# Hybrid decoder block on one core: the first two modulation vectors by quarters instead of halves

## The chip, the cores and the metric

The kernel runs on one core of a Trainium2 chip. The metric is the time of one execution in device microseconds (us). One matmul engine (TensorE, PE in the profile, its weight loads apart as PEld), VectorE (DVE), ScalarE (ACT) and GpSimd (POOL) work side by side; SyncE (SP) issues nearly all transfers.

## The reference

One block of a decoder in float32: 512 tokens of width 1024. What concerns this case is its head:

```python
mod = jax.nn.silu(c) @ w_ada[l] + b_ada[l]
shift1, scale1, gate1, shift2, scale2, gate2 = jnp.split(mod[:, None, :], 6, axis=-1)
h = rms_norm(x, norm1_w[l]) * (1.0 + scale1) + shift1
proj = h @ w_in[l]
aq, ak, av, gq, gk, gv, gg, glr = jnp.split(proj, split_points, axis=-1)
...
mixed = jnp.concatenate([att, go], axis=-1) @ w_out[l]
x = x + gate1 * mixed
```

`c` is one vector of 1024, `w_ada` is 1024 x 6144. `proj` feeds sliding-window attention (8 heads, window 128) and a gated linear attention (GLA, 4 heads, chunks of 64, decays from `glr` by a rank-16 gate). Behind them stand a product-key expert layer with 16384 experts, which takes most of the kernel's time, and a last norm.

## The kernel before

x stays in row blocks of 128 tokens (`gv` and the first half of `Eg`, `xn`); the projections need h transposed, [1024 rows of features, 512 tokens], in 8 blocks `k` of 128 features. Every float32 operand of a projection is split into a high and a low part (`hTh`, `hTl`; `wi_0h`, `wi_0l` for weight blocks 0 to 3, `wi_1h`, `wi_1l` for 4 to 7; `hilo`, L55: ScalarE copies the high part, VectorE subtracts) and each product is three matmuls (`mm3`, L63, lines 64 to 66).

The start-up does this. SP loads x in 8 pieces, then the matrices. ScalarE squares and sums x (L233), `rstd_of` (L71) takes the root on ScalarE and VectorE, ScalarE scales x (L237), and PE transposes it into banks `xt` (L246). `mod_half(v, half)` (L255) makes half of modulation vector 1 (scale) or 0 (shift): it loads 512 output columns of all 8 k blocks (1 MB twice; for v=1 into the ring `raw` of three buffers of 1 MB, for v=0 into `qT` and four `mixA`, which are free then), VectorE multiplies block k by silu(c)'s column k and adds (L267 for the first, L269 for the next 7, into `macc`), four matmuls with a column of ones sum over partitions (L273, into `mt`), and VectorE adds the bias (L275, `modT`) and, for v=1, forms (1+scale) times the norm's weight (L278, `aT`). With both vectors of a half there, four blocks of h follow: ScalarE applies scale and shift (L298; block 7 on VectorE, L300) and copies the high part (L301), VectorE takes the low part (L302). The order is (1,0), (0,0), four h, (1,1), (0,1), four h.

Behind it come the projections, in this order of the program: `decays` (L351: pglr, 16 wide, then `pz` by `gup`, then `la`), projection 3 (gq), projection 4 (gk), projection 0 (queries); one projection has two banks `pj` of 24 matmuls, and pglr has one. Then GLA's preparation (`gla_prep`, L427: 14 products on `Eg`, L451 and L452, then `kl`, L456), attention, projections 5 to 8 (`proj_N`, banks `pn`) between them, and the vectors 2 to 4 (`mod_part`, L202, also through the ring `raw`).

The order of each engine's instructions is not the program's: the tile framework schedules them with a simulated timeline (L38) that has its own durations, so an edit here can turn rows round further on. PSUM tiles come from tags: `m` and the pair `sc2` (`bank2`, L120, one buffer of two banks), `pt`, `po`, and `ph` (`pbank`, L123). A weight load of a projection is issued when its place in the ring of three is free, and SP's queue is taken in order.

Of the kernel before, what the change touches and what calls it, by code (L numbers as in the profile page):

```python
# [41 lines left out]
def peer_block_kernel(ctx: ExitStack, tc: tile.TileContext, a: dict, out: bass.AP):  # L42
# [186 lines left out]
    for n in range(NT):  # L229
        sq = frA.tile([P, D], F32, tag="m4", bufs=2, name=f"sqa{n}")  # L230
        ss = frA.tile([P, 2], F32, tag="ss", bufs=2, name=f"ssa{n}")
        for q in range(2):
            nc.scalar.activation(sq[:, q * 512:(q + 1) * 512], xn[n][q], AF.Square, accum_out=ss[:, q:q + 1])  # L233
        nc.vector.tensor_tensor(ss[:, 0:1], ss[:, 0:1], ss[:, 1:2], OP.add)
        r = rstd_of(frA, ss[:, 0:1], float(D), 1, f"ra{n}")
        for q in range(2):
            nc.scalar.activation(xn[n][q], xn[n][q], AF.Copy, scale=r)  # L237
    xts = []

    def x_transposes(ks):  # L240
# [67 lines left out]
    nc.vector.tensor_tensor(wgl, wg, wgh, OP.subtract)  # L308
    bcast_load(sink, a["sinks"], 8)
# [257 lines left out]
    proj_T(4, [[t[:, :, j, :] for t in gk] for j in range(2)], bank)  # L567
# [523 lines left out]
def layouts(inp):  # L1091
# [6 lines left out]
    o["w_ada"] = c(g["w_ada"][0])  # L1098
# [49 lines left out]
```

## Time and profile before

| | before |
|---|---|
| median of 3 runs (lowest to highest) | 1559.18 us (1557.12 to 1560.58) |
| the profiled execution | 1555.13 us |
| its span in the profile, mean granted clock | 1553.4 us, 0.99 |
| busy: PE, DVE, ACT, POOL | 1493.2, 1251.8, 688.8, 412.9 us |
| the first weight of a modulation vector summed | 13.80 us |
| first matmul of a projection (pglr) | 33.79 us |
| first matmul of projection 0 | 68.22 us |

All times below are from the start of the span. In a row of the timeline the first number is the start of a piece of work, the second what it lasted, in brackets how long the engine was idle before and what ended that. Two or more like instructions in a row share one line with their count; a float32 matmul of one column appears as two records (four matmuls are x8).

### The profile page before, as it was taken

What the parts mean: (1) busy time and instruction counts of PE and PEld (TensorE: products, weight loads), DVE (VectorE), ACT (ScalarE), POOL (GpSimd) and SP (SyncE); (2) the same over time, 40 slices, a digit from 0 to 9 for tenths busy, and PEclk for the clock granted to TensorE, in tenths of its full rate; (3) what the DMA queues carried; (4) which work ended last, traced back from release to release, by engine and by line L of the source; (5) the groups of instructions that cost most, each with busy time, mean ns of one, the idle gap of its engine ahead of it and who ended that gap; (6) DMA issues with size and microseconds to landing.
All of it is one profiled execution on the core that took longest, in us unless ns stands there. A gap on an engine that the chain in (4) does not pass through costs nothing.

```text
span 1553.4 us, 24408 instructions
## 1 busy us (share of the span) xinstructions
PE 1493.2 (96%) x9379; PEld 1328.2 (86%) x9379; DVE 1251.8 (81%) x2476; ACT 688.8 (44%) x1078; POOL 412.9 (27%) x327
## 2 busy tenths in 40 slices
PE   4999989899999999999999999999999999999996
PEld 3787878888998999999888888888888888888885
DVE  7578668589989898995678778878888878887997
ACT  5545576433445666564333333333333333333343
POOL 1000000144500000003243334433434434434550
PEclk9999999999999999999999999999999999999998
DMA  9253444262346677679998999888998989898893
GB/s 349 89 204 131 171 142 173 108 239 92 127 155 188 198 239 235 201 239 388 380 348 317 339 348 346 322 340 333 364 330 329 338 340 354 326 340 334 292 331 129
DMA packets 154932, 409.67 MB, mean 264 GB/s; under 512 B 10288, under 2 KB 77120, under 8 KB 142400
## 3 DMA queue, kind: packets, MB, share of 16 engines
q1 hardware_dynamic: 108736, 261.30, 47.2%
q0 software_dynamic: 36864, 134.23, 23.0%
q10 hardware_dynamic: 9216, 12.59, 2.2%
q8 instruction: 73, 1.20, 0.3%
q14 instruction: 43, 0.35, 0.1%
HBM read 366.14 MB, written 41.94 MB: 263 GB/s over the span
## 4 chain that ended last, share of the span: by engine, by line
PE 63%; DVE 3%; DMA 2%; ACT 1%; issue 1%; DVEq 0%; ACTq 0%; SPq 0%
PE acc L65 11%; PE acc L64 11%; PE acc L66 11%; PE ph L66 8%; PE ph L64 8%; PE ph L65 8%; PE pg L874 4%; DMA Gd<-gs 1%; DMA gr<-Gd 1%; DVE o L867 1%; ACT gs L876 0%; DVE o L862 0%; DVE oh L819 0%; DVE oh L822 0%; DVE oh L817 0%
## 5 line engine op out<-in xcount | busy, mean ns | idle before, releaser
L887 POOL DMA_INDIRECT gu<-in_u_dram,ix_u x128 | 170.2, 1329 | 531.5 <-PE pg L874 273.5
L897 POOL DMA_INDIRECT gv<-in_vP_dram,ix_v x128 | 171.0, 1336 | 214.9 <-DVE gu L889 183.1
L902 DVE SCALAR_TENSOR_TENSOR gacc<-gv,hg,gacc 128x1024 f32<-128x1024 f32 x127 | 162.7, 1281 | 3.3 <-DMA gv<-in_vP_dram,ix_v 3.1
L889 DVE SCALAR_TENSOR_TENSOR gu<-gu,h2n 128x1024 f32<-128x1024 f32 x128 | 156.0, 1219 | 5.9 <-DMA gu<-in_u_dram,ix_u 5.9
L1028 ACT ACTIVATE Ah<-ge 128x384 fp32r<-128x384 f32 x64 | 33.6, 525 | 155.1 <-PE acc L65 155.1
L1028 ACT ACTIVATE Ah<-gel 128x384 fp32r<-128x384 f32 x64 | 33.6, 525 | 154.4 <-PE acc L65 154.4
L876 ACT ACTIVATE gs<-pg 128x512 f32<-128x512 f32 x96 | 94.3, 1108 | 9.8 <-PE pg L874 9.8
L867 DVE TENSOR_TENSOR o<-o,gp 128x1024 bf16<-128x1024 bf16 x144 | 91.0, 687 | 4.3
L874 PE MATMUL pg<-o,o 128*128 128x128 bf16 x1152 | 79.3, 223 | 5.3 <-DVE o L867 5.3
L874 PEld LDWEIGHTS <-o 128*128 128x128 bf16 x1152 | 69.7, 99 | 14.4 <-issue 8.5
L953 POOL IOTA iot<- 128x256 bf16 x1 | 1.5, 1541 | 282.8 <-DVE h2Tl L675 282.8
L1029 DVE TENSOR_TENSOR Al<-gel,Ah 128x384 fp32r<-128x384 f32 x64 | 35.6, 556 | 45.2 <-ACT Ah L1028 45.2
L699 ACT ACTIVATE ge<-ph 128x384 f32<-128x384 f32 x128 | 60.8, 475 | 23.8 <-PE ph L66 23.7
L862 DVE TENSOR_TENSOR o<-iot,t 128x2048 bf16<-128x2048 bf16 x48 | 58.5, 1218 | 4.9 <-ACT t L842 4.9
L1029 DVE TENSOR_TENSOR Al<-ge,Ah 128x384 fp32r<-128x384 f32 x64 | 35.5, 555 | 19.2 <-ACT Ah L1028 18.1
L1024 DVE TENSOR_TENSOR ge<-ge,gr 128x384 f32<-128x384 f32 x64 | 35.4, 553 | 10.9 <-ACT ge L699 10.9
L212 DVE SCALAR_TENSOR_TENSOR macc<-wa,scs,macc 128x1024 f32<-128x1024 f32 x28 | 39.0, 1392 | 4.9 <-DMA wa<-in_w_ada_dram 4.7
L1024 DVE TENSOR_TENSOR gel<-gel,gr 128x384 f32<-128x384 f32 x64 | 32.8, 553 | 0.0
L65 PE MATMUL pq<-h2Tl,wq_0h 128*128 128x512 f32 (+1 forms) x80 | 27.9, 349 | 1.2 <-DVE h2Tl L675 1.2
L64 PE MATMUL pq<-h2Th,wq_0h 128*128 128x512 f32 (+1 forms) x80 | 28.0, 352 | 1.0 <-ACT qha L751 1.0
L65 PE MATMUL pq<-h2Tl,wq_1h 128*128 128x512 f32 (+1 forms) x80 | 28.2, 353 | 0.0
L66 PE MATMUL pq<-h2Th,wq_1l 128*128 128x512 f32 (+1 forms) x80 | 28.2, 352 | 0.0
(2599 smaller groups left out, 5077.1 us busy)
## 6 DMA issues: line engine op xcount, KB each, us to landing
u<-in_uT_dram SPq DMA_DIRECT2D x64, 1024.0 KB
v<-in_vP_dram SPq DMA_DIRECT2D x64, 1024.0 KB
Gd<-gs SPq DMA_DIRECT2D x24, 1024.0 KB
gr<-Gd SPq DMA_DIRECT2D x16, 1536.0 KB
wa<-in_w_ada_dram SPq DMA_DIRECT2D x20, 1024.0 KB
gsp<-ge ACTq DMA_DIRECT2D x64, 192.0 KB
gel<-gsp SPq DMA_DIRECT2D x32, 384.0 KB
wi<-in_w_in_dram SPq DMA_DIRECT2D x9, 1024.0 KB
```

Of the source, the lines that this page charges most:

```text
L64: nc.tensor.matmul(acc, lh, rh, start=start, stop=False)
L65: nc.tensor.matmul(acc, lh, rl, start=False, stop=False)
L66: nc.tensor.matmul(acc, ll, rh, start=False, stop=stop)
L867: nc.vector.tensor_tensor(o2[:, :, m], o12[:, :, 1], gp3[:, g0:g0 + H, m, None].to_broadcast([P, H, P, 2]), OP.mult)
L874: nc.tensor.matmul(pt[:, i, :], o12[:, g, 0, :, r], o2[:, g, m, :, r], start=(m == 0), stop=(m == 2))
L876: nc.scalar.activation(gs[:, :, t0 + 4 * f:t0 + 4 * f + 4].rearrange("p b a -> p a b"), pt, AF.Copy)
L887: nc.gpsimd.indirect_dma_start(out=ur, out_offset=None, in_=a["u"], in_offset=bass.IndirectOffsetOnAxis(ap=ix_u[:, s:s + 1], axis=0))
L889: nc.vector.scalar_tensor_tensor(ur, ur, 1.0, h2n, op0=OP.mult, op1=OP.mult, accum_out=hid[:, s:s + 1])
L897: nc.gpsimd.indirect_dma_start(out=vr, out_offset=None, in_=a["vP"], in_offset=bass.IndirectOffsetOnAxis(ap=ix_v[:, s:s + 1], axis=0))
L902: nc.vector.scalar_tensor_tensor(gacc, vr, hg[:, s:s + 1], gacc, op0=OP.mult, op1=OP.add)
L1024: nc.vector.tensor_tensor(ge, ge, v_part.g[:, :, c % CG, :], OP.mult)
L1029: nc.vector.tensor_tensor(Al, gef, Ah, OP.subtract)
```

## The change

The two vectors are made by quarters of 256 outputs, (1,0), (0,0), (1,1), (0,1) and so on up to (0,3). `w_ada` gets a second copy for them, laid out so that a quarter is one contiguous MB with 8 KB per partition (before, rows of 2 KB). A quarter goes to a place that is free then: A is `qT`, B the four tiles `at` made one, C the second half of `Eg`, or the ring. `mod_quarter` sums 256 columns (the products are lines 248 and 250 of the new kernel), has 2 matmuls with ones (L252), `modT` (L254) and `aT` (L257). x's transposes go by quarters into the pair `sc2` alone (L286), and two h of a quarter follow (L296 and L297 on ScalarE, hTl on VectorE). Of x's scaling the first half goes to VectorE (L276), the second stays on ScalarE (L277); h of block 7 goes to ScalarE. The memsets of `at` and `atc` on POOL move behind. pglr, pz and projection 4 take other banks, so that pglr and the banks of projections 3 and 4 (five) are open at once. The diff:

```diff
--- before.py
+++ after.py
@@ -188,10 +188,9 @@
 
 
 
-    atz = [frG.tile([P, 4, P], F32, name=f"at{i}") for i in range(NT)]
+    ata = frG.tile([P, NT, 4, P], F32, name="at")
+    atz = [ata[:, n] for n in range(NT)]
     atc = [frG.tile([P, 4, 32], F32, name=f"atc{i}") for i in range(2)]
-    for t in atz + atc:
-        nc.gpsimd.memset(t, 0.0)
 
 
     nc.scalar.activation(scs, cT, AF.Exp, scale=-1.0)
@@ -226,86 +225,84 @@
             if v == 4:
                 nc.vector.scalar_tensor_tensor(aT[:, 1, :], modT[:, v * 8:v * 8 + 8], 1.0, n2T, op0=OP.add, op1=OP.mult)
 
+    wraw = {}
+
+    def fetch(src, g, w, name):
+        wraw[name, g] = raw([P, KD, w], f"{name}{g}")
+        nc.sync.dma_start(wraw[name, g], src)
+
+
+    by_k = lambda t: t.rearrange("p (k d) -> p k d", d=256)
+    places = {"A": by_k(qT.rearrange("p a b -> p (a b)")), "B": by_k(ata.rearrange("p n h t -> p (n h t)")),
+              "C": by_k(Eg[:, 4:8, :].rearrange("p a b -> p (a b)"))}
+    quarter = {}
+
+    def fetch_quarter(v, q, place):
+        quarter[v, q] = places[place] if place else raw([P, KD, 256], f"wa{v}{q}")
+        nc.sync.dma_start(quarter[v, q], a["w_ada01"][v, q])
+
+    def mod_quarter(v, q):
+        w = quarter.pop((v, q))
+        pb = mtb[:, 8 * v + 2 * q:8 * v + 2 * q + 2]
+        acc = frA.tile([P, 256], F32, tag="macc", bufs=2, name=f"macc{v}{q}")
+        nc.vector.tensor_scalar(acc, w[:, 0, :], scs[:, 0:1], None, op0=OP.mult)
+        for k in range(1, KD):
+            nc.vector.scalar_tensor_tensor(acc, w[:, k, :], scs[:, k:k + 1], acc, op0=OP.mult, op1=OP.add)
+        for i in range(2):
+            nc.tensor.matmul(pb[:, i:i + 1], acc[:, i * P:(i + 1) * P], ones[:, 0:1], start=True, stop=True)
+        cs = slice(v * 8 + 2 * q, v * 8 + 2 * q + 2)
+        nc.vector.tensor_tensor(modT[:, cs], pb, badaT[:, cs], OP.add)
+        if v == 1:
+            hs = slice(2 * q, 2 * q + 2)
+            nc.vector.scalar_tensor_tensor(aT[:, 0, hs], modT[:, cs], 1.0, n1T[:, hs], op0=OP.add, op1=OP.mult)
+
+    fetch_quarter(1, 0, "A")
+    fetch_quarter(0, 0, "B")
+    fetch(a["w_in"][3], 3, 256, "wi")
+    fetch_quarter(1, 1, "C")
+    wg = frA.tile([P, KD, 16], F32, name="wg")
+    nc.sync.dma_start(wg, a["w_glr"])
+    fetch_quarter(0, 1, None)
+    fetch(a["w_in"][4], 4, 256, "wi")
+
+
     for n in range(NT):
         sq = frA.tile([P, D], F32, tag="m4", bufs=2, name=f"sqa{n}")
         ss = frA.tile([P, 2], F32, tag="ss", bufs=2, name=f"ssa{n}")
-        for q in range(2):
-            nc.scalar.activation(sq[:, q * 512:(q + 1) * 512], xn[n][q], AF.Square, accum_out=ss[:, q:q + 1])
+        nc.scalar.activation(sq[:, 0:512], xn[n][0], AF.Square, accum_out=ss[:, 0:1])
+        nc.scalar.activation(sq[:, 512:1024], xn[n][1], AF.Square, accum_out=ss[:, 1:2])
         nc.vector.tensor_tensor(ss[:, 0:1], ss[:, 0:1], ss[:, 1:2], OP.add)
         r = rstd_of(frA, ss[:, 0:1], float(D), 1, f"ra{n}")
-        for q in range(2):
-            nc.scalar.activation(xn[n][q], xn[n][q], AF.Copy, scale=r)
-    xts = []
-
-    def x_transposes(ks):
-        for k in ks:
-            if k % 4 == 0:
-                x_transposes.two = bank2(f"xt{k}")
-            pt = x_transposes.two[:, k % 4] if k % 4 < 2 else bank(f"xt{k}", ("pt", "po")[k % 2])
-            for n in range(NT):
-                nc.tensor.transpose(pt[:, n * P:(n + 1) * P], xn[n][k // 4][:, k % 4 * P:(k % 4 + 1) * P], ident)
-            xts.append(pt)
-
-    x_transposes(range(4))
+        nc.vector.tensor_scalar(xn[n][0], xn[n][0], r, None, op0=OP.mult)
+        nc.scalar.activation(xn[n][1], xn[n][1], AF.Copy, scale=r)
+    mtb = bank("mt")
     hTh = frA.tile([P, KD, T], FR, name="hTh")
     hTl = frA.tile([P, KD, T], FR, name="hTl")
-
-    mtb = bank("mt")
-
-    def mod_half(v, half):
-        acc = frA.tile([P, D], F32, tag="m4", bufs=2, name=f"macc{v}{half}")[:, :512]
-        c0 = v * D + half * 512
-        if v == 1:
-            parts = [(raw([P, 4, 512], f"wa{half}{i}"), 4) for i in range(2)]
-        else:
-            parts = [(qT, 4)] + [(t.rearrange("p a b -> p (a b)")[:, None, :], 1) for t in mixA]
-        k = 0
-        for w, nk in parts:
-            nc.sync.dma_start(w, a["w_ada"][k * P:(k + nk) * P, c0:c0 + 512].rearrange("(k p) d -> p k d", p=P))
-            for i in range(nk):
-                if k == 0:
-                    nc.vector.tensor_scalar(acc, w[:, i, :], scs[:, 0:1], None, op0=OP.mult)
-                else:
-                    nc.vector.scalar_tensor_tensor(acc, w[:, i, :], scs[:, k:k + 1], acc, op0=OP.mult, op1=OP.add)
-                k += 1
-        pb = mtb[:, 16 * v + 4 * half:16 * v + 4 * half + 4]
-        for i in range(4):
-            nc.tensor.matmul(pb[:, i:i + 1], acc[:, i * P:(i + 1) * P], ones[:, 0:1], start=True, stop=True)
-        cs = slice(v * 8 + 4 * half, v * 8 + 4 * half + 4)
-        nc.vector.tensor_tensor(modT[:, cs], pb[:, 0:4], badaT[:, cs], OP.add)
-        if v == 1:
-            hs = slice(4 * half, 4 * half + 4)
-            nc.vector.scalar_tensor_tensor(aT[:, 0, hs], modT[:, cs], 1.0, n1T[:, hs], op0=OP.add, op1=OP.mult)
-
-    wraw = {}
-
-    def fetch(src, g, w, name):
-        wraw[name, g] = raw([P, KD, w], f"{name}{g}")
-        nc.sync.dma_start(wraw[name, g], src)
-
-    for half in range(2):
-        mod_half(1, half)
-        if half == 1:
-            fetch(a["w_in"][4], 4, 256, "wi")
-        mod_half(0, half)
-        if half == 0:
-            fetch(a["w_in"][3], 3, 256, "wi")
-        else:
-            x_transposes(range(4, KD))
-        for k in range(4 * half, 4 * half + 4):
+    for q in range(4):
+        two = bank2(f"xt{q}")
+        for i in range(2):
+            k = 2 * q + i
+            for n in range(NT):
+                nc.tensor.transpose(two[:, i, n * P:(n + 1) * P], xn[n][k // 4][:, k % 4 * P:(k % 4 + 1) * P], ident)
+        mod_quarter(1, q)
+        if q < 2:
+            fetch_quarter(1, q + 2, "AC"[q])
+        mod_quarter(0, q)
+        if q < 2:
+            fetch_quarter(0, q + 2, ("B", None)[q])
+        for i in range(2):
+            k = 2 * q + i
             h32 = frA.tile([P, T], F32, tag="h32", bufs=4, name=f"h32_{k}")
-            if k < KD - 1:
-                nc.scalar.activation(h32, xts[k], AF.Identity, bias=modT[:, k:k + 1], scale=aT[:, 0, k:k + 1])
-            else:
-                nc.vector.tensor_scalar(h32, xts[k], aT[:, 0, k:k + 1], modT[:, k:k + 1], op0=OP.mult, op1=OP.add)
+            nc.scalar.activation(h32, two[:, i], AF.Identity, bias=modT[:, k:k + 1], scale=aT[:, 0, k:k + 1])
             nc.scalar.activation(hTh[:, k, :], h32, AF.Copy)
             nc.vector.tensor_tensor(hTl[:, k, :], h32, hTh[:, k, :], OP.subtract)
-    wg = frA.tile([P, KD, 16], F32, name="wg")
-    nc.sync.dma_start(wg, a["w_glr"])
     wgh = frA.tile([P, KD, 16], FR, name="wgh")
     wgl = frA.tile([P, KD, 16], FR, name="wgl")
     nc.scalar.activation(wgh, wg, AF.Copy)
     nc.vector.tensor_tensor(wgl, wg, wgh, OP.subtract)
+
+    for t in atz + atc:
+        nc.gpsimd.memset(t, 0.0)
     bcast_load(sink, a["sinks"], 8)
     bcast_load(gnw, a["gnw"], P)
     nc.sync.dma_start(gup, a["gup"])
@@ -350,12 +347,13 @@
 
     def decays():
 
-        pg = pbank("pglr")
+        pg = bank("pglr")
         for k in range(KD):
             mm3(pg[:16, :], wgh[:, k, :], wgl[:, k, :], hTh[:, k, :], hTl[:, k, :], k == 0, k == KD - 1)
         nc.scalar.activation(glrT, pg[:16, :], AF.Copy)
+        pz2 = bank2("pz")
         for j in range(2):
-            pz = bank(f"pz{j}", ("pt", "po")[j])
+            pz = pz2[:, j]
             nc.tensor.matmul(pz, gup[:, j * P:(j + 1) * P], glrT, start=True, stop=True)
             z = frA.tile([P, T], F32, tag="h32", bufs=4, name=f"z{j}")
             e = frA.tile([P, T], F32, tag="h32", bufs=4, name=f"e{j}")
@@ -564,7 +562,7 @@
     mixd, ungated = {}, []
     decays()
     proj_T(3, [[t[:, :, j, :] for t in gq] for j in range(2)], scale=0.125)
-    proj_T(4, [[t[:, :, j, :] for t in gk] for j in range(2)], bank)
+    proj_T(4, [[t[:, :, j, :] for t in gk] for j in range(2)], lambda name: bank(name, ("pt", "po")[int(name[-1])]))
     proj_T(0, (qT[:, 0, :], qT[:, 1, :]), scale=0.125)
     gla_prep(0)
     proj_T(1, (qT[:, 2, :], qT[:, 3, :]), bank, scale=0.125)
@@ -1096,6 +1094,8 @@
     o["x"] = c(g["x"].reshape(T, D))
     o["cT"] = c(g["c"].reshape(KD, P).T)
     o["w_ada"] = c(g["w_ada"][0])
+
+    o["w_ada01"] = c(g["w_ada"][0][:, :2 * D].reshape(KD, P, 2, 4, 256).transpose(2, 3, 1, 0, 4))
     o["b_ada"] = c(g["b_ada"])
     t = lambda v: v.reshape(-1, P).T
     o["vecT"] = c(np.concatenate([t(g["b_ada"][0]), t(g["norm1_w"][0]), t(g["norm2_w"][0]),
```

What the scheduler makes of it, in three places. First PE where the projections begin, before; `mt` are the sums over partitions, `xt` the transposes of x, pj_470 the first bank of projection 3:

```order
L273 MATMUL mt<-ones,macc_276 128x1 x4
L273 MATMUL mt<-ones,macc_295 128x1 x4
L246 MATMUL xt_372<-ident,Eg 128x128 x8
L246 MATMUL xt_381<-ident,Eg 128x128 x4
L246 MATMUL xt_386<-ident,Eg 128x128 x4
L64 MATMUL pglr<-hTh,wgh 16x512
L64 MATMUL pj_470<-hTh,wi_0h 128x512
L65 MATMUL pglr<-hTl,wgh 16x512
L66 MATMUL pglr<-hTh,wgl 16x512
L64 MATMUL pglr<-hTh,wgh 16x512
```

All transposes of x stand ahead of pglr, and then only pglr and one bank run.

The same engine, at the sums of quarter 1 of the shift (macc_326) in the new kernel; pj_498 and pj_525 are the banks of projection 3, pj_560 and pj_587 those of projection 4, macc_357 is scale's quarter 2:

```order
L65 MATMUL pj_587<-hTl,wi_0h 128x512
L66 MATMUL pj_587<-hTh,wi_0l 128x512
L252 MATMUL mt<-ones,macc_326 128x1 x2
L286 MATMUL xt_348<-ident,Eg 128x128 x8
L64 MATMUL pglr<-hTh,wgh 16x512
L64 MATMUL pj_498<-hTh,wi_0h 128x512
L64 MATMUL pj_525<-hTh,wi_0h 128x512
L64 MATMUL pj_560<-hTh,wi_0h 128x512
L64 MATMUL pj_587<-hTh,wi_0h 128x512
L252 MATMUL mt<-ones,macc_357 128x1 x2
L65 MATMUL pglr<-hTl,wgh 16x512
L66 MATMUL pglr<-hTh,wgl 16x512
```

The transposes of the next quarter (xt_348) now stand between the matmuls, and each quarter's rows are taken by all five banks.

PE at the last quarter of the new kernel, macc_412 being shift's quarter 3:

```order
L65 MATMUL pj_560<-hTl,wi_1h 128x512
L66 MATMUL pj_560<-hTh,wi_1l 128x512
L252 MATMUL mt<-ones,macc_412 128x1 x2
L65 MATMUL pj_587<-hTl,wi_1h 128x512
L66 MATMUL pj_587<-hTh,wi_1l 128x512
L64 MATMUL pglr<-hTh,wgh 16x512
L64 MATMUL pj_498<-hTh,wi_1h 128x512
```

Two matmuls of quarter 2 stand behind the last sums, then pglr begins quarter 3.

VectorE at projection 6, before; wi_1414 is its weight, macc_1526 the sum of vector 3, the Eg rows are the products of `gla_prep`:

```order
L210 TENSOR_SCALAR macc_1526<-wa_0_1527,scs 128x1024
L60 TENSOR_TENSOR wi_1l<-wi_1414,wi_1h 128x1024
L212 SCALAR_TENSOR_TENSOR macc_1526<-wa_0_1527,scs,macc_1526 128x1024
L396 TENSOR_REDUCE mx_1320<-sc_1312 128x2
L396 TENSOR_REDUCE mx_1320<-sc_1313 128x2
L212 SCALAR_TENSOR_TENSOR macc_1526<-wa_2_1531,scs,macc_1526 128x1024
L397 TENSOR_TENSOR mx_1320<-mx_1320,sink 128x4
L451 TENSOR_TENSOR Eg<-Eg,gq_107 128x4x64
L452 TENSOR_TENSOR Eg<-Eg,gk_108 128x4x64
L451 TENSOR_TENSOR Eg<-Eg,gq_107 128x8x32
```

The same in the new kernel, where the weight is wi_1442 and the sum macc_1554:

```order
L450 TENSOR_TENSOR Eg<-Eg,gk_108 128x128x2
L449 TENSOR_TENSOR Eg<-Eg,gq_107 128x256
L450 TENSOR_TENSOR Eg<-Eg,gk_108 128x256
L454 TENSOR_TENSOR kl_1195<-Eg,gk_108 128x512
L219 TENSOR_TENSOR gate1b<-ba_1330,gb_1335 128x512
L209 TENSOR_SCALAR macc_1554<-wa_0_1555,scs 128x1024
L401 TENSOR_TENSOR Z_1350<-Z_1350,es_1351 128x4
L60 TENSOR_TENSOR wi_1l<-wi_1442,wi_1h 128x1024
L394 TENSOR_REDUCE mx_1399<-sc_1391 128x2
```

The second low half of projection 6 stood ahead of the products of Eg; now it stands behind the last of them, `kl`, gate1b and the first product of the sum.

## Rows read from the trace of the kernel before

**Rows 1.** Page: busy time of each engine, and the shares of the last chain.
```profile
PE 1493.2 (96%) x9379; PEld 1328.2 (86%) x9379; DVE 1251.8 (81%) x2476; ACT 688.8 (44%) x1078; POOL 412.9 (27%) x327
...
PE 63%; DVE 3%; DMA 2%; ACT 1%; issue 1%; DVEq 0%; ACTq 0%; SPq 0%
```

**Rows 2.** Windows: us; busy PE, PEld, DVE, ACT, POOL (count); PEclk, DMA share, GB/s.
```profile
10.00:20.00 10.00, 3.45 (x13) 2.25 (x14) 6.82 (x25) 7.34 (x19) 0.00 (x0) 1.00 1.05 392
20.00:30.00 10.00, 4.38 (x21) 4.20 (x19) 9.65 (x17) 3.24 (x5) 0.00 (x0) 1.00 1.05 389
30.00:40.00 10.00, 9.54 (x42) 7.19 (x42) 9.79 (x16) 4.88 (x8) 0.00 (x0) 1.00 1.04 408
40.00:50.00 10.00, 8.19 (x43) 6.30 (x41) 5.41 (x11) 3.36 (x6) 0.00 (x0) 1.00 0.21 86
```

**Rows 3.** Timeline of the start, all engines, to the first matmul of projection 0.
```profile
13.80 0.49 DVE L267 TENSOR_SCALAR macc<-wa,scs 128x512 f32<-128x512 f32 x1 [0.33 <-DMA wa<-in_w_ada_dram]
...
28.96 2.79 ACT L298 ACTIVATE h<-xt,modT,aT 128x512 f32<-128x512 f32 x4 [1.56 <-DVE modT L275]
...
30.46 3.67 PE L246 MATMUL xt<-ident,Eg 128*128 128x128 f32 x16 [2.39 <-ACT h L298]
33.79 0.78 PE L64 MATMUL pglr<-hTh,wgh 128*16 128x512 f32 x1
...
39.92 0.95 PE L273 MATMUL mt<-ones,macc 128*128 128x1 f32 x8
...
43.00 0.50 PE L66 MATMUL pj<-hTh,wi_0l 128*128 128x512 f32 x1 [1.56 <-DVE wi_0l L60]
...
46.38 0.16 DVE L275 TENSOR_TENSOR modT<-mt,vec 128x4 f32<-128x4 f32 x1 [1.99 <-PE mt L273]
...
48.65 2.19 ACT L301 ACTIVATE hTh<-h 128x512 fp32r<-128x512 f32 x4
49.31 2.50 DVE L302 TENSOR_TENSOR hTl<-h,hTh 128x512 fp32r<-128x512 f32 x4 [1.92 <-ACT hTh L301]
...
60.05 1.98 PE L359 MATMUL pz<-glrT,gup 16*128 16x512 f32 x4
...
68.22 0.39 PE L64 MATMUL pj<-hTh,wi_0h 128*128 128x512 f32 x1
```

**Rows 4.** Groups of VectorE by form up to 260 us: busy, mean ns, idle before.
```profile
L269 DVE SCALAR_TENSOR_TENSOR macc<-wa,scs,macc 128x512 f32<-128x512 f32 x14 | 10.5, 748 | 0.2
...
L406 DVE TENSOR_SCALAR sS<-sS,Z 128x256 f32<-128x256 f32 x24 | 6.8, 349 | 0.1
...
L302 DVE TENSOR_TENSOR hTl<-h,hTh 128x512 fp32r<-128x512 f32 x8 | 5.1, 686 | 1.9 <-ACT hTh L301 1.9
...
L369 DVE SCALAR_TENSOR_TENSOR la<-z,e 128x256 f32<-128x256 f32 x4 | 1.5, 423 | 12.1 <-ACT e L365 12.1
```

**Rows 5.** Windows, with the granted clock: an idle stretch, and after a later pause.
```profile
24.00:26.00 2.00, 0.00 (x0) 0.00 (x0) 1.93 (x3) 0.80 (x1) 0.00 (x0) 1.00 1.05 386
151.00:152.00 1.00, 1.00 (x7) 1.00 (x6) 1.00 (x2) 0.34 (x1) 0.00 (x0) 0.50 0.04 12
153.00:154.00 1.00, 1.00 (x6) 1.00 (x6) 1.00 (x4) 0.97 (x5) 0.00 (x0) 0.50 0.65 147
154.00:155.00 1.00, 1.00 (x11) 0.87 (x12) 1.00 (x2) 1.00 (x6) 0.00 (x0) 0.85 1.06 438
```

**Rows 6.** Timeline of the later stage: projection 6, Eg's products, projection 7.
```profile
130.48 1.22 DVE L60 TENSOR_TENSOR wi_1l<-wi,wi_1h 128x1024 fp32r<-128x1024 f32 x1
...
135.28 0.42 DVE L451 TENSOR_TENSOR Eg<-Eg,gq 128x256 f32<-128x256 f32 x1
...
139.97 0.68 DVE L456 TENSOR_TENSOR kl<-Eg,gk 128x512 f32<-128x512 f32 x1
...
146.75 1.06 ACT L59 ACTIVATE wi_0h<-wi 128x1024 fp32r<-128x1024 f32 x1 [2.76 <-DMA wi<-in_w_in_dram]
...
149.63 0.21 PE L493 MATMUL pa<-gq,gk 64*32 64x32 f32 x1 [2.11 <-issue]
```

More of the change, by code (lines that the diff above doesn't have):

```diff
@@ L227, in mod_part @@
                 nc.vector.scalar_tensor_tensor(aT[:, 1, :], modT[:, v * 8:v * 8 + 8], 1.0, n2T, op0=OP.add, op1=OP.mult)
-    for n in range(NT):
-        sq = frA.tile([P, D], F32, tag="m4", bufs=2, name=f"sqa{n}")
-        ss = frA.tile([P, 2], F32, tag="ss", bufs=2, name=f"ssa{n}")
-        for q in range(2):
-            nc.scalar.activation(sq[:, q * 512:(q + 1) * 512], xn[n][q], AF.Square, accum_out=ss[:, q:q + 1])
-        nc.vector.tensor_tensor(ss[:, 0:1], ss[:, 0:1], ss[:, 1:2], OP.add)
-        r = rstd_of(frA, ss[:, 0:1], float(D), 1, f"ra{n}")
-        for q in range(2):
-            nc.scalar.activation(xn[n][q], xn[n][q], AF.Copy, scale=r)
@@ L238, in peer_block_kernel @@
-    xts = []
-    def x_transposes(ks):
-        for k in ks:
-            if k % 4 == 0:
-                x_transposes.two = bank2(f"xt{k}")
-            pt = x_transposes.two[:, k % 4] if k % 4 < 2 else bank(f"xt{k}", ("pt", "po")[k % 2])
-            for n in range(NT):
-                nc.tensor.transpose(pt[:, n * P:(n + 1) * P], xn[n][k // 4][:, k % 4 * P:(k % 4 + 1) * P], ident)
-            xts.append(pt)
-    x_transposes(range(4))
-    hTh = frA.tile([P, KD, T], FR, name="hTh")
-    hTl = frA.tile([P, KD, T], FR, name="hTl")
@@ new lines, in peer_block_kernel @@
+    fetch_quarter(1, 0, "A")
[7 more added lines that the diff above has]
+    for n in range(NT):
+        sq = frA.tile([P, D], F32, tag="m4", bufs=2, name=f"sqa{n}")
+        ss = frA.tile([P, 2], F32, tag="ss", bufs=2, name=f"ssa{n}")
+        nc.scalar.activation(sq[:, 0:512], xn[n][0], AF.Square, accum_out=ss[:, 0:1])
+        nc.scalar.activation(sq[:, 512:1024], xn[n][1], AF.Square, accum_out=ss[:, 1:2])
+        nc.vector.tensor_tensor(ss[:, 0:1], ss[:, 0:1], ss[:, 1:2], OP.add)
+        r = rstd_of(frA, ss[:, 0:1], float(D), 1, f"ra{n}")
+        nc.vector.tensor_scalar(xn[n][0], xn[n][0], r, None, op0=OP.mult)
+        nc.scalar.activation(xn[n][1], xn[n][1], AF.Copy, scale=r)
@@ new lines, in peer_block_kernel @@
+    mtb = bank("mt")
+    hTh = frA.tile([P, KD, T], FR, name="hTh")
+    hTl = frA.tile([P, KD, T], FR, name="hTl")
+    for q in range(4):
+        two = bank2(f"xt{q}")
+        for i in range(2):
+            k = 2 * q + i
+            for n in range(NT):
+                nc.tensor.transpose(two[:, i, n * P:(n + 1) * P], xn[n][k // 4][:, k % 4 * P:(k % 4 + 1) * P], ident)
[7 more added lines that the diff above has]
+            k = 2 * q + i
```

## The prediction

> **What bounds the kernel now.** I read the page first: busy shares and the chain that ended last. PE is busy for 1493.2 of 1553.4 us, 96%, and holds 63% of that chain [rows 1]. So the time moves almost only by what PE waits for, and the change can matter only where PE is not full: at the start, until the projections run, and in a few pauses later. The windows of the first 50 us come next [rows 2]: from 10 to 30 us PE is busy for 3.45 and 4.38 of each 10 us while the loads run at 389 to 392 GB/s, and from 30 us on it is nearly full. The timeline gives the order of that stretch [rows 3]: the first sum on VectorE at 13.80, the first four h on ScalarE at 28.96, sixteen transposes on PE in the gap at 30.46, the first projection matmul (pglr) at 33.79, and the first matmul of projection 0 at 68.22. The lines of VectorE give the price of each kind of sum [rows 4]; windows around one later pause show PE's clock [rows 5], and its timeline the engines there [rows 6].
>
> The yardstick is the start of projection 0: by then before and after have done the same work (three projections, all of h, the gates' pz). The trace is of an execution of 1555.13 us (span 1553.4, 1.7 around it); the median of the runs is 1559.18, 4.05 above. I make the sum as a difference and add it to the median. About 0.2%, 3.1 us, is what a measurement of this kernel can tell from no change.
>
> **The change part by part.**
>
> *The start of the projections.* Before, PE's first pglr waits for two sums of 512 columns, 8 products each at 0.748 us [rows 4], with wi 3's halves between them, then the h: 33.79. Now only two sums of 256 columns are due. A 256-column product of this form takes 0.423 and the first of a sum (no addend) about 0.349, the nearest rows of that size [rows 4]. The sums start as before at 13.8, when the first MB is down [rows 3]. Up to the end of the second sum VectorE holds 16 products (2 x 0.349 + 14 x 0.423 = 6.6), the two lo halves of wi 3 (2 x 1.22, as one at 130.48 [rows 6]) and two scalings of x with the small operations of the norm (about 2.0): 11.0. Successors begin some 0.08 before an end (four hTl of 0.686 took 2.50 [rows 3, 4]), 27 times: -2.2; ScalarE's cast of wi 3 is half a microsecond late: +0.5. The second sum ends at 13.8 + 9.3 = 23.1. Two mt matmuls cost 0.5 (four: 0.95 [rows 3]); modT stands behind rows of the next sum on VectorE: 0.9; two h on ScalarE 1.4 (four: 2.79); the first transposes are already done for quarter 0, but eight of quarter 1 stand in PE's row ahead of pglr, 8 x 0.23 = 1.85, as 16 took 3.67 [rows 3]. That is 27.8: **-6.0 us**.
>
> *Work put behind that start.* Before, all 32 transposes precede pglr and so do 8 of the 16 mt matmuls. Now 16 transposes and 12 mt matmuls stand among the projections, where PE is full: 3.67 + 4 x 0.24 = **+4.6**.
>
> *Pauses of PE in the three projections.* From 33.79 to 68.22 are 34.4 us. Five banks take 24 matmuls each, 120 x 0.229 = 27.5 (16 transposes in 3.67 and 42 records in 9.54 busy us [rows 2, 3] give the same price); with 8 mt matmuls 1.9 and pz 1.98 that is 31.4, so PE paused for 3.0, half of it at 43.00, where it waited 1.56 for wi's lo half [rows 3]. Now the whole chain of a quarter lies inside: mt on PE, modT on VectorE, h on ScalarE, the transposes of the next quarter into the one pair of banks of tag sc2, which are free only when both h have read it. In PE's new row the mt matmuls of quarter 1 are followed directly by transposes that need that pair: modT 0.16 with its hand-off and two h, 1.9 us with nothing else in the row. The same at quarter 2, behind one projection's rows: 1.4. At the end mt of quarter 3, then modT 0.2, two h 1.4 and hTh 0.55 (four: 2.19 [rows 3]), less two matmuls still in the row, with the hand-off 1.8. One wait for a weight's lo half: 0.5 by adding up VectorE's row (1.56 before). Pauses 5.6 in place of 3.0, **+2.6**; bounds: +1.0, if VectorE and ScalarE run ahead and only the bank pair costs, and +4.5, if each hand-off costs the 1.92 to 2.39 that the rows show behind modT, hTh and h [rows 3].
>
> *VectorE's own work.* 64 products of 256 for 32 of 512: 56 x 0.423 + 8 x 0.349 = 26.5 against 28 x 0.748 + 4 x 0.49, 22.9 [rows 3, 4]; and half of x's scaling comes to it, while h_7 goes to ScalarE. From 20 to 40 us it is busy for 9.65 and 9.79 of 10 us [rows 2], which seems to leave nothing. But the sums of quarters 1 to 3, added up from these durations row by row, end an estimated 2 to 4 us before PE reaches their mt matmuls (the nearest is scale's quarter 2, 38.5 against 40.7), since PE now has three projections' rows to run between. That is the cover: nothing is charged. If it goes, each microsecond that VectorE is late is one of PE.
>
> *Transfers.* The same bytes; quarters are contiguous, 8 KB per partition. A MB takes 2.7 us at 389 to 408 GB/s [rows 2]. SP's queue has wg and the fetches of wi 3, wi 4 in another order; quarter 3's loads wait for places freed by sums of quarters 0 and 1, and land at 33 to 38 us, before their sums. ScalarE loses four half scalings and gains h_7: below 1 us, beside 3.24 busy of 10 [rows 2]. POOL's memsets, moved behind, are needed by attention at about 100 us: nothing.
>
> *The later stage.* The new durations turn the scheduler's rows over down to about 200 us. The place that matters is projection 6. Before, its second lo half runs at 130.48, ahead of the 14 gating products of Eg (135.28 to 139.97, 4.7 us) [rows 6]. Now it stands behind them, kl, gate1b and the first product of the third vector. The products move up by the 1.2 it leaves: 139.97 - 1.2, then kl 0.68, the other two some 0.7 each, itself 1.22, and the later start 1.1 (less overlaps): it ends at about 142.4. PE's row ahead of projection 6, counted by the durations of before, ends at an estimated 138.7: a new pause of 3.7. Against it, the pause that ends at 149.63, 2.11 us, behind wi 7's late load (ScalarE waits 2.76 for it at 146.75 [rows 6]), goes, as projection 7 now comes behind attention's matmuls. After that pause the granted clock was 0.50, the lower of its two levels (1.2 of 2.4 GHz), in 151 to 154, and 0.85 in the next us [rows 5]: 3 x 0.5 + 0.15 = 1.7 us of work lost, gone with it. Net 3.7 - 3.8 = **-0.1**. Bounds: -3.8 (only the old one goes) and +3.7 (only the new one comes).
>
> Sum: -6.0 + 4.6 + 2.6 - 0.1 = **+1.1**; I take +1.5, since the prices of the hand-offs lie below the waits that the rows show. Forecast 1559.18 + 1.5 = **1560.7 us**: a start of 6 us sooner that is given back inside the projections.
>
> **Rivals.**
>
> *The new pause comes and the old one stays.* Projection 6's lo half is late behind the Eg products, and wi 7's load, bound to a ring of three buffers that projection 6 frees later, is late too. For: VectorE's row has the lo half behind 4.7 us of products, and the ring is the same. Against: PE reaches the place about 1 us later, and projection 7 has attention's matmuls ahead. It decides if PE is at its first matmul before about 139. Price: the 3.8 stays: 1.5 + 3.8 = +5.3, **1564.5**, slower.
>
> *The clock.* After the pause of 2.11 us the clock fell for 3 us, 1.7 us lost [rows 5, 6]. Now PE has three hand-offs of 1.4 to 1.9 at the start; if two of them cost a fall, 1.5 + 3.4 = +4.9: **1564.1**. For: that pause. Against: from 24 to 26 us PE did nothing and the granted clock was 1.00 [rows 5], and the pause of 1.56 at 43.00 lies in a stretch that shows 1.00 [rows 2, 3]. The Trainium skill, TensorE: Matmul & The Clock Gate, section What's actually happening, says that an idle PE gets only half of its clock pulses until it has been busy again; by that rule, with a fall behind each of the three hand-offs, the sum would be 1.5 + 3 x 1.7 = +6.6, by the idle stretch at 24 us it stays +1.5; this trace shows both outcomes after idle time, a fall and none.
>
> *The gain is kept.* The new pause is not there (the lo half of projection 6 is ready because PE comes there later, with attention's rows drawn ahead), the old one is gone with its half clock, and hand-offs cost their lower bound: 1.5 - 3.7 (the later stage at -3.8 for -0.1) - 1.6 (pauses +1.0 for +2.6) = -3.8, **1555.4**, faster. For: the start is sure to be earlier, and the later stage is one of exchange. Against: it asks two things that the rows don't show.
>
> **How the numbers follow.** Forecast 0.42 (its own range 1558.0 to 1563.0: the bounds of the pauses, -1.6 and +1.9 about their value, and half a microsecond of the later stage), the new pause 0.24, the clock 0.10, the gain kept 0.24. Faster by over 0.2%: 0.19 of the last and 0.02 of the forecast: 0.21. Slower: 0.22 of the new pause, 0.06 of the clock, 0.07 of the forecast: 0.35. Within: the rest, 0.44. Range 1554.5 to 1567.0: below it lies the gain kept by another microsecond (0.08 left out), above it both slower rivals together (0.10).
>
> **What would show it.** Right: the first pglr matmul at about 28; PE pauses behind mt of quarters 1 to 3 that sum to 5 to 6 us; projection 0 at 69 to 71; a pause of 3 to 4 us at about 139 to 142 that ends by VectorE's lo half, and none near 148; clock 1.00 up to 100 us. Wrong: sums on VectorE ending after PE's need (mt waits "for macc" by more than 1 us), or quarters that land late (waits of sums for the DMA), which would make pauses above 8; or projection 0 before 67.

## The result and the profile after

| | before | after |
|---|---|---|
| median (lowest to highest) | 1558.15 us (1555.13 to 1560.58), 4 runs | 1581.85 us (1576.04 to 1583.02), 4 runs |
| ratio to before, 95% interval | | 1.0149, 1.0128 to 1.0170 |
| the profiled execution, its span, mean clock | 1555.13, 1553.4 us, 0.99 | 1583.02, 1581.2 us, 0.979 |

The change costs 23.7 us. The forecast was 1560.7 with a range up to 1567.0: wrong, by a size that none of its rivals had. Of the page of the changed kernel, parts 1 and 4, answering to [rows 1]:

```profile
PE 1506.7 (95%) x9379; PEld 1337.9 (85%) x9379; DVE 1258.8 (80%) x2517; ACT 683.8 (43%) x1072; POOL 406.5 (26%) x327
...
PE 59%; DVE 5%; DMA 3%; issue 1%; ACT 1%; DVEq 0%; ACTq 0%
```

PE's busy time has grown by 13.5 us although it does the same 9379 instructions: a slower clock shows up as busy time. The two profiled executions are the fastest of the kernel before and the slowest of the changed one, 27.8 us apart by their spans, so parts read from them add up to more than the 23.7 us of the medians.

First the start, where the forecast looked. Windows of the changed kernel (columns as in [rows 2]):

```profile
10.00:20.00 10.00, 3.25 (x11) 1.97 (x11) 8.15 (x32) 6.48 (x17) 0.00 (x0) 1.00 1.02 426
20.00:30.00 10.00, 4.46 (x18) 3.78 (x18) 9.93 (x24) 4.28 (x7) 0.00 (x0) 1.00 1.00 409
30.00:40.00 10.00, 8.21 (x45) 6.56 (x44) 7.66 (x21) 2.46 (x4) 0.53 (x1) 1.00 0.80 331
40.00:50.00 10.00, 9.28 (x40) 7.05 (x37) 7.96 (x19) 2.02 (x3) 1.57 (x3) 0.83 0.01 2
```

The loads are done by 40 us, but PE is busy for 8.21 where it was busy for 9.54, and from 40 to 50 the granted clock is 0.83. PE's timeline of the changed kernel there:

```profile
26.98 1.97 PE L286 MATMUL xt<-ident,gv 128*128 128x128 f32 x8 [1.92 <-ACT h L296]
28.60 0.77 PE L64 MATMUL pglr<-hTh,wgh 128*16 128x512 f32 x1
...
39.04 1.09 PE L286 MATMUL xt<-ident,Eg 128*128 128x128 f32 x8 [1.79 <-ACT h L296]
...
50.27 0.61 PE L252 MATMUL mt<-ones,macc 128*128 128x1 f32 x4 [0.99 <-DVE modT L254]
51.74 1.09 PE L286 MATMUL xt<-ident,Eg 128*128 128x128 f32 x8 [0.87 <-ACT h L296]
...
61.84 0.40 PE L64 MATMUL pglr<-hTh,wgh 128*16 128x512 f32 x1 [1.67 <-ACT hTh L297]
...
68.82 1.12 PE L357 MATMUL pz<-glrT,gup 16*128 16x512 f32 x2
69.87 0.50 PE L64 MATMUL pj<-hTh,wi_0h 128*128 128x512 f32 x1
...
71.00 1.12 PE L357 MATMUL pz<-glrT,gup 16*128 16x512 f32 x2
```

The first pglr comes at 28.60 (forecast 27.8, before 33.79 [rows 3]); behind it stand the three waits of the transposes and of pglr for h and hTh (1.79, 0.87 and 1.67) and one for modT (0.99), 5.3 us in all. Projection 0 begins at 69.87 with one half of pz left (71.00 to 72.05): 70.9 at equal work against 68.22, **+2.7**, where the sum had +1.2 without the later stage's -0.1. Projection 2 ends 2.2 us later than before (103.70 against 101.48 for the last low-part matmul). So some 21 us of the medians' 23.7 have another source, behind the projections. Windows from 70 us to the first matmul of the second stage's query projection (`pq`); the kernel before, then the changed one:

```profile
70.00:271.70 201.70, 193.32 (x1984) 159.66 (x1983) 149.83 (x321) 119.95 (x260) 0.00 (x0) 0.98 0.46 163
```

```profile
70.00:294.10 224.10, 207.95 (x1993) 169.17 (x1993) 155.21 (x330) 123.33 (x272) 0.00 (x0) 0.92 0.43 149
```

That stretch is 22.4 us longer, with the start's 2.7 in it. PE does the same work in it (1984 and 1993 records, of which a few are missing), but it is idle for 16.2 instead of 8.4 us, and busy for 14.6 us more, as the mean clock is 0.92 instead of 0.98 (0.08 of 224.1 less 0.02 of 201.7: 13.9). Nearly two thirds of the loss are clock, a third pauses. (The other 5.4 of the 27.8 us lie behind the first `pq`; they are not traced here.) Where the clock falls in the changed kernel, and what PE did before:

```profile
116.00:120.00 4.00, 2.77 (x21) 1.82 (x21) 1.94 (x8) 2.21 (x12) 0.00 (x0) 0.86 0.28 114
120.00:124.00 4.00, 4.00 (x25) 3.60 (x24) 1.90 (x9) 2.88 (x13) 0.00 (x0) 0.50 0.00 0
136.00:140.00 4.00, 1.81 (x16) 1.71 (x15) 0.55 (x2) 4.00 (x4) 0.00 (x0) 1.00 0.00 0
144.00:148.00 4.00, 4.00 (x27) 3.65 (x26) 4.00 (x8) 0.00 (x0) 0.00 (x0) 0.50 0.00 0
164.00:168.00 4.00, 2.32 (x46) 2.13 (x46) 2.80 (x4) 0.60 (x1) 0.00 (x0) 0.84 1.03 368
168.00:172.00 4.00, 4.00 (x40) 2.27 (x38) 2.90 (x3) 0.60 (x1) 0.00 (x0) 0.50 1.03 356
176.00:180.00 4.00, 2.71 (x26) 2.47 (x25) 2.47 (x8) 2.57 (x6) 0.00 (x0) 1.00 0.99 361
...
200.00:204.00 4.00, 4.00 (x19) 3.63 (x19) 0.24 (x2) 0.00 (x0) 0.00 (x0) 0.60 0.00 0
...
228.00:232.00 4.00, 1.81 (x8) 0.95 (x8) 3.87 (x4) 3.98 (x6) 0.00 (x0) 0.94 0.13 10
232.00:240.00 8.00, 5.82 (x31) 4.36 (x32) 4.73 (x7) 3.94 (x7) 0.00 (x0) 0.50 0.95 318
```

Four times a stretch of half-busy PE (2.77, 1.81, 2.32 and 1.81 of 4 us) stands ahead of one at 0.50, the lower of the two levels (1.2 of 2.4 GHz), as the pause in [rows 5, 6] did. The kernel before has two such places up to 240 us (the other stands ahead of 212 us), and the clock stays low for a shorter time there. This is no rule without exceptions: behind 176 to 180 us, 2.71 busy, no fall follows at once, and at 200 to 204 us the clock falls behind a full PE. Three of PE's pauses ahead of these stretches, from its timeline:

```profile
117.22 0.27 PE L382 MATMUL sc<-am,identb 128*128 128x256 bf16 x1 [1.57 <-ACT sS L398]
...
140.38 0.38 PE L382 MATMUL sc<-am,identb 128*128 128x512 bf16 x1 [2.57 <-ACT sS L398]
...
167.08 0.25 PE L488 MATMUL pa<-Eg 64*32 64x16 f32 x5 [1.68 <-issue]
```

The one at 140.38 stands where the forecast put a pause, but it is not the lo half of projection 6 that ends it. PE waits for ScalarE's `sS`, and ScalarE has the Abs and the Exp of Eg (3.17 and 3.62 us, lines 443 and 444) ahead of it, the Exp directly:

```profile
131.18 3.17 ACT L443 ACTIVATE Eg<-Eg 128x3584 f32<-128x3584 f32 x1
...
135.80 3.62 ACT L444 ACTIVATE Eg<-Eg 128x4096 f32<-128x4096 f32 x1
```

And the end of attention, all engines:

```profile
233.42 1.12 PE L419 MATMUL po<-PT,vN 128*64 128x128 f32 x8 [3.27 <-ACT PT L414]
...
234.50 2.13 DVE L558 TENSOR_TENSOR al<-mixA,ah 128x512 fp32r<-128x512 f32 x3
...
237.44 0.60 ACT L422 ACTIVATE mixA<-po 128x512 f32<-128x512 f32 x1 [1.22 <-PE po L419]
...
238.99 0.69 DVE L558 TENSOR_TENSOR al<-mixA,ah 128x512 fp32r<-128x512 f32 x1 [2.36 <-ACT ah L557]
```

PE waits 3.27 us for attention 3's PT with nothing beside it. All four `al`, the low parts of attention's output for the output projection (`pw`), run here, three in a row at 234.50 and the last behind mixA of block 3. Before, they were spread. VectorE's `al`, count, durations, first and last start, of the kernel before and of the changed one:

```profile
L560 DVE TENSOR_TENSOR al<-mixA,ah x4: 683/684/693, 141.9 to 231.0; 128x512 fp32r<-128x512 f32 x4
```

```profile
L558 DVE TENSOR_TENSOR al<-mixA,ah x4: 681/692/693, 234.5 to 239.0; 128x512 fp32r<-128x512 f32 x4
```

`al` takes its buffers from the tag of mixA, five buffers for mixA 0 to 3 and one more. Before, the start loaded half of vector 0 into the four mixA tiles, so that they had their buffers from the first microseconds on. The change loads into `at` (place B) instead, and the mixA tiles are first touched in attention. This became theory A: in the scheduler's timeline `al` of block 0 queues for a buffer behind mixA of block 3, and so the scheduler draws another order. On the chip it is the order that holds them: three `al` start at 234.50, ahead of block 3's mixA at 237.44. Theory B: whatever draws it, the new order behind projection 0 is the loss. Theory C, the rival from the forecast: the start's pauses and its clock are the loss.

### The profile page after: what moved, and what is told of

The parts are those of the page before. It is cut to its first block, busy times and chain, and to the rows that moved or that the text cites. A ratio compares the mean times of both kernels' runs of the same rounds, so it can differ in the third digit from the quotient of the medians.

```text
span 1581.2 us, 24422 instructions
## 1 busy us (share of the span) xinstructions
PE 1506.7 (95%) x9379; PEld 1337.9 (85%) x9379; DVE 1258.8 (80%) x2517; ACT 683.8 (43%) x1072; POOL 406.5 (26%) x327
## 3 DMA queue, kind: packets, MB, share of 16 engines
q0 software_dynamic: 36864, 134.23, 22.9%
## 4 chain that ended last, share of the span: by engine, by line
PE 59%; DVE 5%; DMA 3%; issue 1%; ACT 1%; DVEq 0%; ACTq 0%
PE acc L65 11%; PE acc L64 11%; PE acc L66 11%; PE ph L64 8%; PE ph L66 8%; PE ph L65 8%; PE pg L872 3%; DVE o L865 2%; DMA u<-in_uT_dram 1%; DVE o L860 1%; DMA gr<-Gd 1%; DMA gu<-in_u_dram,ix_u 0%; DVE oh L817 0%; DVE oh L815 0%; ACT gs L874 0%
## 5 line engine op out<-in xcount | busy, mean ns | idle before, releaser
L885 POOL DMA_INDIRECT gu<-in_u_dram,ix_u x128 | 166.8, 1303 | 531.0 <-DVE o L865 271.6
```

The costliest lines, as they stand in the source:

```text
L885: nc.gpsimd.indirect_dma_start(out=ur, out_offset=None, in_=a["u"], in_offset=bass.IndirectOffsetOnAxis(ap=ix_u[:, s:s + 1], axis=0))
```

## The experiments

Every kernel here computes the whole block. "Late order" means that the instructions of each engine from projection 0 on are tied to the order that another kernel has there, by edges that fix only the order of issue.

**1. mixA touched at the start.**

```diff
+    for t in mixA: nc.gpsimd.memset(t, 0.0)
```

> The changed kernel with one thing added: four memsets on POOL that touch the mixA tiles at the start, so that al of block 0 need not queue behind mixA of block 3 for a buffer of their common tag. Theory A (the late al is what costs): al of blocks 0 to 2 moves from 234 us back to 140 to 200, PE no longer stands at half load at 228 to 236 us, and the time falls from 1582 by 8 to 12, to 1570 to 1574. Theory B (the whole order behind projection 0 costs, of which al is a part): the rows before 190 us stay as they are, so their pauses and falls of the clock stay, and the time ends between 1565 and 1575. Theory C (the start itself costs): no change, 1578 to 1583.

Measured: 1568.87 us against 1556.73, ratio 1.0077 (1.0049 to 1.0105). About half of the loss goes with four memsets off PE's path. `al` starts at 131.7 to 250.8, and from 228 to 236 us PE is busy for 7.00 of 8 us instead of 3.98. The rows up to 160 us stay (clock 0.72 at 120 to 130, 0.66 at 140 to 150). Behind them the order differs, and run 1 has a fall of its own: 0.51 at 180 to 190, where the changed kernel has 1.00. The time lies in B's range and just below A's. A holds for the end of attention; C, which asked for no change, cannot explain it.

**2. The start of before, the late order of the changed kernel.** In these lines `at` is a list of places in the program, not the tile.

```diff
...
+        for p, n in zip(at, at[1:]):
+            tc.add_manual_dep(traced[n], traced[p].name, free, reason="keep_order")
```

> The kernel before, with every engine's instructions from projection 0 on put into the order that they have in the changed kernel (order edges without waits); the start up to there is that of before. Theory B (the order behind projection 0 is what costs): 1574 to 1580, with falls of the clock at about 116 to 124, 140 to 148, 164 to 172 and 230 to 240 us as in the changed kernel. Theory A (only the late al): 1566 to 1572. Theory C (the start costs): within 3 us of before, 1555 to 1561.

Measured: 1575.42, ratio 1.0120 (1.0086 to 1.0155). The start of the kernel before with only the order changed loses 18.7 us: theory B. The clock falls at 110 to 130, 140 to 150, 160 to 180 and 230 to 240 us.

**3. The changed start (mixA touched early), the late order of before.** The same edges, with the other order.

> The changed kernel with the four memsets on mixA and every engine's instructions from projection 0 on in the order of the kernel before. Theory B (the order behind projection 0 is what costs): the start's own +2 to +3 us are left, 1559 to 1563. Theory C (the start costs, by hand-offs and by the clock): 1574 to 1582. Theory A alone: 1570 to 1574.

Measured: 1566.25, ratio 1.0065 (1.0039 to 1.0091): +9.5 where B expected +2 to +3. Most of the loss goes, but more stays than the start shows, and no theory had this time. Part of it lies at projection 0, see runs 7 and 8.

**4. The kernel before, with `at` in place of mixA at the start.** The smallest edit that makes mixA late (with it, the memsets of `at` stand behind the loads); no quarters, no new banks.

```diff
-            parts = [(qT, 4)] + [(t.rearrange("p a b -> p (a b)")[:, None, :], 1) for t in mixA]
+            parts = [(qT, 4)] + [(t.rearrange("p a b -> p (a b)")[:, None, :], 1) for t in atz]
```

> The kernel before with one thing changed: the second half of vector 0's loads goes to the four at tiles in place of the four mixA tiles (memsets moved behind), so that mixA's buffers are first taken in attention, as in the changed kernel. Theory A: al of all blocks bunches behind attention 3, at 215 to 230 us, and the time rises by 6 to 12, to 1564 to 1570. Theory B: a rise of 3 to 20 according to how far the order is redrawn. Theory C: no change, 1555 to 1561.

Measured: 1579.60, ratio 1.0125 (1.0084 to 1.0167): **+22.9 by one name** (13 to 26 by the interval), about as much as the whole change, and more than A alone expected. `al` of that run, and its window from 70 us to the first pq:

```profile
L561 DVE TENSOR_TENSOR al<-mixA,ah x4: 681/692/693, 230.5 to 236.0; 128x512 fp32r<-128x512 f32 x4
```

```profile
70.00:291.20 221.20, 205.98 (x1983) 169.22 (x1981) 152.93 (x324) 122.12 (x263) 0.00 (x0) 0.92 0.44 151
```

Idle 15.2 us and a clock of 0.92: the changed kernel's sums, without its start. The places are others: PE's order is that of before up to about 147 us, and the clock falls at 150 to 180 us (0.66, 0.58 and 0.74) and at 230 to 240 (0.50). So run 4 does not repeat the changed kernel's order; that the two lose about the same is in part chance.

**10. The same with mixA touched early** (told here since it is run 4's counterpart).

```diff
+    for t in atz + atc + mixA: nc.gpsimd.memset(t, 0.0)
```

> The run with at for mixA in the kernel before (+23), with mixA also touched by memsets at the start. Every engine's order from projection 0 on is then that of before. Theory A and B: all of the +23 goes, 1555 to 1561. If the at tiles or the memsets moved behind cost something by themselves: above 1564.

Measured: 1558.51 against 1556.84, ratio 1.0017 (0.9997 to 1.0037): all of it is gone. Every engine's order behind projection 0 is that of before again, and so are the rows:

```profile
L561 DVE TENSOR_TENSOR al<-mixA,ah x4: 687/691/696, 141.3 to 229.8; 128x512 fp32r<-128x512 f32 x4
```

```profile
70.00:270.40 200.40, 191.91 (x1984) 158.25 (x1983) 149.78 (x321) 119.76 (x260) 0.00 (x0) 0.99 0.47 164
```

Runs 4 and 10 differ in when four tiles are first touched, and in the order that follows from it. That makes A the cause of run 4's new order, and that order the cause of its time. In the changed kernel A is only a part: run 1 takes back 11 (by the ratios) to 13 us (by the medians).

**5. Place B in mixA.** Four loads of two k blocks each in place of one load into `at`, which is four tiles again.

```diff
...
-    places = {"A": by_k(qT.rearrange("p a b -> p (a b)")), "B": by_k(ata.rearrange("p n h t -> p (n h t)")),
+    places = {"A": by_k(qT.rearrange("p a b -> p (a b)")), "B": [t.rearrange("p h (b d) -> p (h b) d", b=1).rearrange("p (k c) d -> p k (c d)", c=2) for t in mixA[:NT]],
...
```

> The changed kernel with its place B moved from the at tiles (which are separate tiles again) to the four mixA tiles, each taking two k blocks of a quarter, so that mixA's buffers are taken at the start as before; no memset on mixA. Theory A (mixA's late buffers cost, through al and through the order that the scheduler then draws): like the run with early memsets, 1563 to 1572, al spread over 130 to 250 us. If the one tile at was what cost: below 1562. If neither: 1578 to 1583.

Measured: 1565.11, ratio 1.0059 (1.0034 to 1.0084). Repairing the place, with the order left to the scheduler, takes back 14 (by the ratios) to 17 (by the medians) of the 23.7 us, as A expected; the change is still slower than before.

**6. mixA early, and the banks of before** (pglr in ph, pz in pt and po, projection 4 in m).

> The changed kernel with mixA touched early and with the banks of before for pglr, pz and projection 4, so that quarters remain but the three projections no longer take each quarter at once. If the five banks at once cost (projection 0 then waits for the copy of projection 3): below the run with early memsets by 3 to 6, 1562 to 1566. If they save pauses: 2 to 6 above it, 1571 to 1575. If only the order counts: anywhere in 1560 to 1575, with more or less time lost by the granted clock between 70 us and the first pq.

Measured: 1569.40, ratio 1.0085 (1.0064 to 1.0106), the same as run 1. With the order free this says nothing on the five banks: PE waits elsewhere (3.9 us for a copy of Eg, 4.7 us at `pa`).

**7 and 8. Two more starts under the late order of before**, both with mixA touched early, as in run 3. Run 7: projections 0 and 1 exchange their banks (ph and m); run 8: the banks of before.

> The changed kernel with mixA touched early and the late order of before, as in the third run, and projection 0 in the banks of tag m, projection 1 in those of tag ph (exchanged). Theory D (the early start and the late order of before meet badly at projection 0, whose banks wait 2.4 us for the copies of projection 3, with a fall of the clock behind it): 4 below that run, 1561 to 1563. Without D: within 1.5 of it, 1565 to 1568.

> The quarters with the banks of before, mixA touched early, and the late order of before. Theory B and D together: no wait at projection 0, the start costs 2 to 3 us and the rest runs as before: 1557 to 1562. Theory C (the quarters' start itself costs more): 1564 to 1570.

Measured: run 7 1570.20, ratio 1.0089 (1.0069 to 1.0109); run 8 1561.61, ratio 1.0022 (1.0008 to 1.0037). Run 8 lies where B and D together had it. Run 7 missed: the wait for the banks went and a longer one for a weight's lo half came in its place. But runs 8, 3 and 7 now have the same late order (but for run 7's first rows) and three pauses at projection 0, of no length, 2.36 and 5.20 us. The longer two, run 3 then run 7:

```profile
73.55 0.80 PE L64 MATMUL pj<-hTh,wi_0h 128*128 128x512 f32 x1 [2.36 <-ACT gq L331]
```

```profile
81.82 0.79 PE L66 MATMUL pj<-hTh,wi_1l 128*128 128x512 f32 x1 [5.20 <-DVE wi_1l L60]
```

The window 60 to 100 us of runs 8, 3 and 7 (columns as in [rows 2]):

```profile
60.00:100.00 40.00, 40.00 (x185) 31.68 (x184) 25.92 (x45) 23.39 (x32) 0.00 (x0) 1.00 0.33 117
```

```profile
60.00:100.00 40.00, 35.73 (x157) 27.12 (x158) 23.16 (x44) 25.03 (x34) 0.00 (x0) 0.96 0.19 66
```

```profile
60.00:100.00 40.00, 33.85 (x135) 24.91 (x133) 20.80 (x40) 26.25 (x35) 0.00 (x0) 0.91 0.21 71
```

In these 40 us idle time and clock cost 0, 4.3 + 1.6 = 5.9 and 6.2 + 3.6 = 9.8 us; 1.9 of run 3's idle time are waits ahead of projection 0. In these windows PE's idle time cost its own length and, by the clock, between a third and over a half of it again. The medians are 1561.6, 1566.3 and 1570.2, 0, 4.7 and 8.6 apart, but that they agree so well is in part luck: by the same matmuls runs 3 and 7 lie 2.3 and 5.1 us behind run 8 at 100 us, and 8.7 and 7.4 at 123 us, behind a further pause each (1.94 and 2.16 us) that run 8 does not have there.

Runs 6 and 8 differ in the late order alone, 1569.40 and 1561.61 us. With them the loss parts in three: mixA touched late, 11 to 13 us (run 1); the order that the quarters draw even with mixA early, 7.8 us (run 6 against run 8); and the start itself, 3.2 us (run 8).

**9. Transposes of quarters 1 and 3 in pt and po**, on run 8.

```diff
...
-        two = bank2(f"xt{q}")
+        two = bank2(f"xt{q}") if q % 2 == 0 else [bank(f"xt{q}{t}", t) for t in ("pt", "po")]
...
```

> The run with old banks and the late order of before, with the transposes of quarters 1 and 3 in the banks pt and po in place of the one pair sc2, so that they no longer wait until both h of the quarter before have read it. If those waits (5.7 us in three, behind them a fall of the clock at 47 to 51 us that costs 1.7) are what the early start loses: 4 to 7 below that run, 1554 to 1558, at or below the kernel before. If PE has no other work in those gaps and waits for h and its high part in their place: within 2 of it, 1559 to 1563.

Measured: 1562.67, ratio 1.0040 (1.0026 to 1.0055), no better than run 8. The transposes' waits for h shrink from 5.6 us (1.92, 1.79 and 1.93) to 3.0 (1.91 and 1.12), but PE now waits 4.2 for sums of VectorE, where run 8 waits 1.4: the quarter's chain is late by itself, the bank only showed it. No version of the quarters came below the kernel before, so the gain of the early pglr seems lost to the chain that ends with the last quarter; no run shortens that chain.

## Why the prediction was wrong

- *The start, -6.0, +4.6, +2.6*: right. pglr at 28.60 for 27.8; the waits behind it 5.3 us in place of 5.6; projection 0 at +2.7 for +1.2. The fall of the clock at 40 to 50 us, 1.7 us of work, was not in the sum. VectorE's product of 256 columns took more than the nearest row said, 0.480 for 0.423, as this group of the changed kernel shows:

```profile
L250 DVE SCALAR_TENSOR_TENSOR macc<-qT,scs,macc 128x256 f32<-128x256 f32 x14 | 6.7, 480 | 0.1
```

- *VectorE's sums are covered*: right. The nearest one, scale's quarter 2, was there before PE; none of PE's waits behind the first pglr (0.87 to 1.79) is for a sum.
- *Transfers: the same bytes, nothing*: right for the loads, and **here the step failed**. I asked when the places A, B and C become free, and never what else the old places had done. Giving up mixA was read as free; in the kernel before run 4 prices it at 22.9 us and run 10, with the tiles touched early, at 1.7; in the changed kernel it is 11 to 13 (run 1).
- *The later stage, -0.1, bounds -3.8 and +3.7*: wrong. I compared rows at one place, projection 6, and took the other changes of order for a wash. Run 2 measures them: +18.7. The bounds came from two pauses of before, but a new order draws new pauses: 16.2 us idle in place of 8.4, at places that no row of before shows. The old pause was not gone either: in the `pa` of the same block PE now waits 1.68 us (the row at 167.08), and the clock falls there (0.84, then 0.50). So the first rival, the new pause beside the old one, came true in kind, with PE waiting for `sS` and not for VectorE's lo half. And wi 7's load was no shown cause of the old pause: the work behind it is `pa`, of gq and gk, and its row names no wait [rows 6].
- *The clock rival*: right in kind and wrong in place. I gave it 0.10 and three pauses at the start. One fall there (0.83 from 40 to 50 us) came; the larger part of the loss, 14.6 of 22.4 us in the stretch behind 70, is the clock too. The Trainium skill, TensorE: Matmul & The Clock Gate, section HAM oscillation — how this bites in real kernels, tells of a kernel that pays for its waits again in throttled time behind each of them; runs 8, 3 and 7 agree, with 1.6 us on 4.3 and 3.6 on 6.2.
- *The gain is kept*: no run showed it.

What stays open: which of the redrawn rows cost how much. Runs 1, 6 and 8 part the loss in three, and no run parts it further; the order within the attention stage was not tried row by row.

## What to carry to other kernels

Where a scheduler orders the engines, ask of each buffer that a change stops using who shares its tag, and who queues behind its first use: touching four tiles early was worth 21 us in one kernel (run 4 against run 10) and 11 to 13 in the other (run 1). Compare the new order over the whole stage, not at one place, and price a redrawn order by its pauses and by the clock behind them: 1.4 to 1.6 us for each us of idle time from 60 to 100 us in runs 3 and 7, but nearly 3 (22.4 on 7.8) over the whole stage of the changed kernel, where PE is half busy around its pauses. A start that is 5 us sooner is worth nothing if the last link, here the last quarter's sums, is not.

## What the runs showed of the hardware

Within one kernel the executions differ with the mean granted clock: the changed kernel took 1576.04 us at 0.983 and 1583.02 at 0.979, and 0.004 of 1580 us is 6.3. The order of the engines' instructions, with the same work but for four memsets on GpSimd, moved this kernel between 1558.5 and 1579.6 us (runs 10 and 4). The product of 256 columns on VectorE takes 0.480 us and that of 512 0.748 [rows 4], so halving a row costs 0.21 more in all.
